# Last FFN: the second product by Strassen's algorithm, with sums made by adding DMAs

## The chip, the cores and the metric

One core of a Trainium2 chip. The metric is the device time of one launch in microseconds (us). The core has engines that run side by side, each with its own queue in program order: TensorE (PE: matmuls, into PSUM), VectorE (DVE), ScalarE (ACT), GpSimd (Pool) and SyncE (SP). DMAs are issued from a queue of SP, ACT or Pool, and are carried by the same 16 DMA engines.

## The reference

A trunk of two layers over 512 tokens of width 1024; each layer is a token mixer and then a dense SwiGLU FFN. The change is in the FFN of the second layer, which is the last thing computed:

```python
D_FF = 2816
def swiglu_ffn(h, w_in, w_out):
    gate, up = jnp.split(h @ w_in, 2, axis=-1)
    return (jax.nn.silu(gate) * up) @ w_out
...
    y = swiglu_ffn(h, f_w_in[i], f_w_out[i])
    x = x + gate * rmsnorm(y, norm_g[i, 3])
```

`h` is [512, 1024], `w_in` [1024, 5632], `w_out` [2816, 1024], all float32. The first product gives gate and up, the second takes their gated product to the output.

## The kernel before

Every operand of a matmul is split in two float32r parts, a high part (a copy that rounds, on ACT) and a low part (the rest, a subtraction on DVE), and each product is three matmuls: high x high, high x low, low x high. The moving operand is 512 wide.

The first product runs over 44 chunks of 128 columns of `w_in` (22 of gate, 22 of up). Each chunk (`in_chunk`) is 8 blocks of the contraction x 3 matmuls into one PSUM bank, with `h` as moving operand. The weights come by SP's queue (`load_w`, 1 MB each, two buffers `wst`) and are split into tiles `whl` (four buffers, `split_w`). `ff_act` makes silu(gate) x up and splits it into 22 tiles `ff`.

The second product is made by `out_begin` and `out_finish`: 2 halves of the output (512 columns) x 22 blocks of the contraction x 4 tiles of 128 tokens x 3 matmuls (`mm_tiles`, lines 378 to 380), the activations as stationary operand. Weights come by `load_wo` (L233) and are split at L203 and L204. The last blocks are left for `finish`, where each token tile is ended in turn (`m0 sq0 b1 yg0 m1a m1b sq1 yg1 rt1 rc1 x0 x1`): squares of the row on ACT (L427), root (L441, ACT) and reciprocal (L444, DVE), product with the gate (L431, DVE), the update of x (L448, DVE) and the store (L450, L457). In this stage the order on PE, ACT and DVE is the program's; elsewhere in `ffn` a scheduler orders them. Pool does nothing here. The launch line gives Pool's DMA descriptors a scratch of 1024 bytes per partition (`dynamic_dma_scratch_size=1024`).

## Time and profile before

| | |
|---|---|
| median of 3 runs | 1366.4 us (1366.18 to 1366.81) |
| profiled execution: its time / its span | 1366.3 us / 1364.5 us |
| TensorE busy | 1353.1 us (99%) |
| DVE / ACT / Pool busy | 849.5 / 539.6 / 11.6 us |
| last FFN, second product: first to last matmul | 1238.54 to 1357.99 us |
| last matmul's end to the span's end | about 1358.4 to 1364.5 us |

The span runs from the first to the last instruction. Rows of groups give line, engine, operation, output<-inputs, shapes and count, then busy time and the mean duration of one in ns, then the idle time ahead of them and what ended it. Durations of matmuls overlap, so their pace is read from start to start. Rows of stretches give the busy time of PE, PE's weight loads, DVE, ACT and Pool with counts, then the granted clock of TensorE (1.00 is full), the mean busy share of the DMA engines, and what they moved in GB/s. Rows of the timeline give start, duration, engine, line and operation.

### The profile page before, as it was taken

What the parts mean: (1) busy time and instruction counts of PE and PEld (TensorE: products, weight loads), DVE (VectorE), ACT (ScalarE), POOL (GpSimd) and SP (SyncE); (2) the same over time, 40 slices, a digit from 0 to 9 for tenths busy, and PEclk for the clock granted to TensorE, in tenths of its full rate; (3) what the DMA queues carried; (4) which work ended last, traced back from release to release, by engine and by line L of the source; (5) the groups of instructions that cost most, each with busy time, mean ns of one, the idle gap of its engine ahead of it and who ended that gap; (6) DMA issues with size and microseconds to landing.
All of it is one profiled execution on the core that took longest, in us unless ns stands there. A gap on an engine that the chain in (4) does not pass through costs nothing.

```text
span 1364.5 us, 17280 instructions
## 1 busy us (share of the span) xinstructions
PE 1353.1 (99%) x6975; PEld 1139.0 (83%) x6975; DVE 849.5 (62%) x1344; ACT 539.6 (40%) x826; POOL 11.6 (1%) x23
## 2 busy tenths in 40 slices
PE   8999999999999999999999999999999999999998
PEld 6788889888888888898888888888898888888886
DVE  5578766787776322759988898897672333333224
ACT  5333355222322222745655545464572232222112
POOL 0000000000000000000000000000000000000000
PEclk9999999999999999999999999999999999999999
DMA  9767750777776232325343433313502332222221
GB/s 311 233 182 241 230 198 17 251 227 246 223 241 215 97 111 90 108 62 160 108 140 110 138 97 105 131 60 119 184 27 83 107 105 98 93 93 93 93 93 62
DMA packets 154212, 190.35 MB, mean 140 GB/s; under 512 B 5892, under 2 KB 111252, under 8 KB 153108
## 3 DMA queue, kind: packets, MB, share of 16 engines
q1 hardware_dynamic: 149984, 176.34, 40.8%
q10 hardware_dynamic: 4148, 12.90, 3.1%
q8 instruction: 55, 0.90, 0.3%
q14 instruction: 25, 0.20, 0.0%
HBM read 186.98 MB, written 2.24 MB: 139 GB/s over the span
## 4 chain that ended last, share of the span: by engine, by line
PE 97%; SPq 2%; DMA 1%; ACT 0%; DVE 0%; issue 0%; DVEq 0%; ACTq 0%
PE ip L276 18%; PE ip L278 18%; PE ip L277 18%; PE y L378 9%; PE y L380 9%; PE y L379 9%; PE li L276 3%; PE li L278 3%; PE li L277 3%; PE li L756 1%; PE yd L1313 1%; SPq L611 1%; PE yo L1307 1%; PE xtr L494 1%; DMA ada_st<-in_ada_w_dram 1%; PE cb L1252 1%
## 5 line engine op out<-in xcount | busy, mean ns | idle before, releaser
L276 PE MATMUL ip<-h,whl 128*128 128x512 f32 x1096 | 430.8, 393 | 0.2 <-DVE cv L863 0.2
L278 PE MATMUL ip<-h,whl 128*128 128x512 f32 x1096 | 426.8, 389 | 0.0
L277 PE MATMUL ip<-h,whl 128*128 128x512 f32 x1096 | 426.5, 389 | 0.0
L276 PEld LDWEIGHTS ip<-h,whl 128*128 128x128 f32 x1096 | 205.8, 188 | 43.9 <-issue 1.8
L278 PEld LDWEIGHTS ip<-h,whl 128*128 128x128 f32 x1096 | 205.7, 188 | 43.3
L277 PEld LDWEIGHTS ip<-h,whl 128*128 128x128 f32 x1096 | 205.8, 188 | 41.8
L204 DVE TENSOR_TENSOR whlo<-wsto,whlo 128x1024 fp32r<-128x1024 f32 x63 | 76.9, 1224 | 162.8 <-ACT whlo L203 162.7
L222 DVE TENSOR_TENSOR whl<-wst,whl 128x1024 fp32r<-128x1024 f32 x96 | 116.7, 1221 | 59.8 <-ACT whl L221 59.6
L378 PE MATMUL y<-whlo,ff 128*128 128x512 f32 x352 | 137.1, 390 | 0.0
L380 PE MATMUL y<-whlo,ff 128*128 128x512 f32 x352 | 136.9, 389 | 0.0
L379 PE MATMUL y<-whlo,ff 128*128 128x512 f32 x352 | 136.9, 389 | 0.0
L203 ACT CAST whlo<-wsto 128x1024 fp32r<-128x1024 f32 x63 | 65.8, 1051 | 162.6 <-PE y L380 149.5
L204 DVE TENSOR_TENSOR whl<-wst,whl 128x1024 fp32r<-128x1024 f32 (+1 forms) x77 | 72.7, 973 | 87.4 <-ACT whl L203 87.4
L124 DVE SCALAR_TENSOR_TENSOR ada_acc<-ada_st,csil,ada_acc 128x512 f32<-128x512 f32 x140 | 105.0, 750 | 4.0 <-DMA ada_st<-in_ada_w_dram 0.5
L221 ACT CAST whl<-wst 128x1024 fp32r<-128x1024 f32 x96 | 99.8, 1041 | 4.1 <-DMA wst<-in_m_w_in_dram 2.4
L203 ACT CAST whl<-wst 128x1024 fp32r<-128x1024 f32 (+1 forms) x77 | 62.6, 846 | 91.1 <-PE ip L278 39.8
L276 PE MATMUL li<-h,whl 128*128 128x256 f32 x288 | 83.2, 289 | 0.0
L278 PE MATMUL li<-h,whl 128*128 128x256 f32 x288 | 81.6, 283 | 0.0
L277 PE MATMUL li<-h,whl 128*128 128x256 f32 x288 | 81.5, 283 | 0.0
L380 PEld LDWEIGHTS y<-whlo,ff 128*128 128x128 f32 x352 | 66.1, 188 | 13.8
L379 PEld LDWEIGHTS y<-whlo,ff 128*128 128x128 f32 x352 | 66.1, 188 | 13.7
L378 PEld LDWEIGHTS y<-whlo,ff 128*128 128x128 f32 x352 | 66.1, 188 | 13.5
(235 smaller groups left out, 1643.9 us busy)
## 6 DMA issues: line engine op xcount, KB each, us to landing
ada_st<-in_ada_w_dram SPq DMA_DIRECT2D x96, 512.0 KB, 5.1
wst<-in_f_w_in_dram SPq DMA_DIRECT2D x44, 1024.0 KB, 5.2
wsto<-in_f_w_out_dram SPq DMA_DIRECT2D x20, 1024.0 KB, 5.0
wst<-in_m_w_in_dram SPq DMA_DIRECT2D x14, 1024.0 KB, 5.4
wst<-in_m_w_in_dram SPq DMA_DIRECT2D x20, 512.0 KB, 5.3
wst<-in_a_w_in_dram SPq DMA_DIRECT2D x9, 1024.0 KB, 6.0
csb<-cs_d ACTq DMA_DIRECT2D x8, 1024.0 KB, 5.1
wsto<-in_m_w_out_dram SPq DMA_DIRECT2D x7, 1024.0 KB, 6.4
```

What stands on the lines that cost most here:

```text
L124: dve.scalar_tensor_tensor(acc, w, csil[:, k:k + 1], acc, MUL, ADD)
L203: act.copy(dst[:, 0, :nk, :], src)
L204: dve.tensor_tensor(dst[:, 1, :nk, :], src, dst[:, 0, :nk, :].bitcast(F32), SUB)
L221: later.append((lambda sw=sw, w=w: act.copy(w[:, 0, :nk, :], sw), lambda sw=sw, w=w: dve.tensor_tensor(w[:, 1, :nk, :], sw, w[:, 0, :nk, : ...
L222: lambda sw=sw, w=w: dve.tensor_tensor(w[:, 1, :nk, :], sw, w[:, 0, :nk, :].bitcast(F32), SUB)))
L276: pe.matmul(dst, w_at(w, 0, kk), a[:, 0, sl], start=start, stop=False)
L277: pe.matmul(dst, w_at(w, 0, kk), a[:, 1, sl], start=False, stop=False)
L278: pe.matmul(dst, w_at(w, 1, kk), a[:, 0, sl], start=False, stop=stop)
L378: pe.matmul(pst, a[:, 0, tk], wt[:, 0, kk, :], start=k == 0, stop=False)
L379: pe.matmul(pst, a[:, 0, tk], wt[:, 1, kk, :], start=False, stop=False)
L380: pe.matmul(pst, a[:, 1, tk], wt[:, 0, kk, :], start=False, stop=k == K - 1)
L494: pe.transpose(pt[:, j * 256 + t * P:j * 256 + (t + 1) * P], self.xn[2 * hi + t][p // 2][:, c:c + P], ident)
```

## The change

The second product is made by Strassen's algorithm in the form that needs seven products of half the size in each dimension. The contraction is parted by blocks: `a?1` and `b1?` are the even blocks of 128, `a?2` and `b2?` the odd ones, 11 of each ("p"). `a1?` are tokens 0 to 255, `a2?` tokens 256 to 511; `b?1` and `b?2` are the two halves of the output's columns. The seven products (`PRODUCTS`) are walked in 77 pairs of product and p, two pairs to a step, 39 steps; a step is 12 matmuls of 512 columns (2 pairs x 2 token tiles x 3 parts). They add into four pairs of PSUM banks, A, B, C and D (one bank for each of the two token tiles), with A taking four of the seven.

The sums of operands are made in place. Of the activations, two are made by DVE (`s13`), and two by DMAs that add (`add_`, issued by Pool): a11 += s1 when product 0 has split its block, a12 += a11 when product 1 has. Of the weights, all four are made by such DMAs: `t1` (b12 += b11), `t3` (b11 is loaded again with the columns of b12 by SP, then b11 += b22), `t2_` (b22 += b12) and `t4` (b21 += b22). They go by units: p = 0 and 1 together, 2 and 3 together, then each p for itself, nine units. The weights of blocks p = 7 to 10 are loaded into the tiles of `h` once the first product has read these, 16 loads of a quarter each.

`behind(n)` is what is issued behind the matmuls of step n; then the weights of step n + 4 (`w_prep`) and the activations of step n + 3 (`a_prep`) are split, from four `whl` and three `ao` buffers. The first two token tiles (c11, c12) are finished at steps 28 to 30, the last two after the last products. The order on all engines is now the program's in the whole FFN.

```diff
-        def ffn(s, i, begun, act_tile, gg_tile, xn_tile, lead, after):
...
+    PRODUCTS = (("A", "b11", "a11"), ("B", "b21", "a12"), ("C", "b22", "a12"), ("A", "b22", "a11"),
+                ("D", "b12", "s1"), ("A", "b11", "a21"), ("A", "b21", "a22"))
-        actp3 = ph.enter_context(tc.tile_pool(name="actp3", bufs=22, reuse_waits="tile"))
-        ffn(3, 1, begun, lambda n: actp3.tile([P, 2, T], F32R, tag="a", name=n),
-            lambda: actp3.tile([P, D], F32, tag="gg", name="gg", bufs=1), None, None, None)
+        fo = ph.enter_context(tc.tile_pool(name="fo", bufs=3, reuse_waits="tile"))
+        fb = ph.enter_context(tc.tile_pool(name="fb", bufs=1, reuse_waits="tile"))
+        h, lead_ps, rest, more = begun
+        w1, w2 = f_w_in[1], f_w_out[1]
+        NP = NF // 2
+        ws, splits, gates = list(more), [(), ()], {}
+        w2t = [fb.tile([P, 2, 2, D], F32, tag=f"w2t{i}", name=f"w2t{i}") for i in range(2)]
+        w2t += [fb.tile([P, 1, 2, D], F32, tag="w2t2", name="w2t2")]
+        raw = fb.tile([P, NF, T], F32, tag="raw", name="raw")
+        s1t = fb.tile([P, NP, 256], F32, tag="s1t", name="s1t")
+        units = [(0, 1), (2, 3)] + [(p,) for p in range(4, NP)]
+        unit_of = {p: i for i, u in enumerate(units) for p in u}
...
+        def w2_load(i):
+
+            u = units[i]
+            t = w2t[i] if i < 3 else wst_p.tile([P, 1, 2, D], F32, tag="wst", name="w2s")
+            for q in range(len(u)):
+                dma(t[:, q, :, :], w2_rows(u[q])[:, 0])
+            rows_of[i] = (t[:, :, 0, :], t[:, :, 1, :])
...
+        def add_(dst, src):
+            pool.dma_start(dst, src, accum_op=ADD)
...
+        def s13(p, n):
+            dve.tensor_tensor(a_("s1", p, n), a_("a21", p, n), a_("a22", p, n), SUB)
+            dve.scalar_tensor_tensor(a_("a21", p, n), a_("a11", p, n), -1.0, a_("a21", p, n), MUL, SUB)
...
+        even = list(range(NP))
+        odd = [4, 0, 1, 2, 3] + list(range(5, NP))
+        steps = [(i, p) for i in range(7) for p in (odd if i % 2 else even)]
+        NT = (len(steps) + 1) // 2
...
+        def w_prep(n):
+            w = whl_p.tile([P, 2, 2, T], F32R, tag="whl", name="whlo")
+            part = steps[2 * n:2 * n + 2]
+            us = {unit_of[p] for _, p in part}
+            if len(us) == 1 and len(part) == 2:
+                todo = [(slice(0, 2), b_(us.pop(), PRODUCTS[part[0][0]][1]))]
+            else:
+                todo = [(slice(q, q + 1), b_(unit_of[p], PRODUCTS[i][1])[:, units[unit_of[p]].index(p):][:, :1])
+                        for q, (i, p) in enumerate(part)]
+            for sl, srcw in todo:
+                act.copy(w[:, 0, sl, :], srcw)
+                dve.tensor_tensor(w[:, 1, sl, :], srcw, w[:, 0, sl, :].bitcast(F32), SUB)
+            w_of[n] = w
+
+        def a_prep(n):
+            a = fo.tile([P, 2, 2, 256], F32R, tag="ao", name="ao")
...
+                    act.copy(a[:, 0, sl, :], srca)
+                    dve.tensor_tensor(a[:, 1, sl, :], srca, a[:, 0, sl, :].bitcast(F32), SUB)
+            for _, (i, p), m in todo:
+                if i == 0:
+                    add_(a_("a11", p, m), a_("s1", p, m))
+                elif i == 1:
+                    add_(a_("a12", p, m), a_("a11", p, m))
+            a_of[n] = a
+
+        def products(tiles):
+            for sub in range(2):
+                for n in tiles:
+                    for q, (i, p) in enumerate(steps[2 * n:2 * n + 2]):
+                        r = PRODUCTS[i][0]
+                        if r not in bank:
+                            bank[r] = [(mm_ps if r == "C" else aux_ps)(f"c{r}{t}") for t in range(2)]
+                        first = i == {"A": 0, "B": 1, "C": 2, "D": 4}[r] and p == (odd if i % 2 else even)[0]
+                        last = p == (odd if i % 2 else even)[-1]
+                        w, a, tk = w_of[n], a_of[n], slice(sub * P, (sub + 1) * P)
+                        for k, (hl, al) in enumerate(((0, 0), (1, 0), (0, 1))):
+                            pe.matmul(bank[r][sub], a[:, al, q, tk], w[:, hl, q, :],
+                                      start=first and k == 0, stop=last and k == 2, skip_group_check=True)
...
+            def t1(i):
+                add_(b_(i, "b12"), b_(i, "b11"))
+
+            def t3(i):
+                u = units[i]
+                for q, p in enumerate(u):
+                    dma(b_(i, "b11", q), w2_rows(p)[:, 0, 0, T:])
+                add_(b_(i, "b11"), b_(i, "b22"))
+
+            def t2_(i):
+                add_(b_(i, "b22"), b_(i, "b12"))
+
+            def t4(i):
+                add_(b_(i, "b21"), b_(i, "b22"))
...
+                if k in (8, 14, 20):
+                    w2_load((8, 14, 20).index(k))
+                if k in (K - 4, K - 2):
+                    w2_load(3 + (k - K + 4) // 2)
+                if k in (K - 12, K - 10, K - 8):
+                    t1((k - K + 12) // 2)
+                tiles.append(in_chunk(ws[k], h))
...
+                    a_prep(k - K + 2)
+                    w_prep(k - K + 2)
+            up(NF - 1, tiles[-1])
+
+            ht = [hp.tile([P, 1, D], F32, tag=f"h{j}", name=f"w2h{j}") for j in range(KD)]
+            for i in range(5, len(units)):
+                rows_of[i] = (ht[2 * (i - 5)], ht[2 * (i - 5) + 1])
+            for c, r in ((0, 0), (0, 1), (1, 0), (1, 1)):
+                for i in range(5, len(units)):
+                    dma(rows_of[i][r][:, 0, c * T:(c + 1) * T], w2_rows(units[i][0])[:, 0, r, c * T:(c + 1) * T])
+            for n in (2, 3):
+                w_prep(n)
+            a_prep(2)
+            for i in range(3, len(units)):
+                t1(i)
...
+            def behind(n):
+
+                if n == 2:
+                    for i in range(len(units)):
+                        t3(i)
+                for i, u in enumerate(units):
+                    if n - 8 == u[-1] // 2:
+                        t2_(i)
+                if n == 18:
+                    for i in range(len(units)):
+                        t4(i)
+                for t in range(2):
+                    if n == 5:
+                        got["11", t] = t2("c11")
+                        act.copy(got["11", t], bank["A"][t])
+                    elif n == 10:
+                        dve.tensor_add(got["11", t], got["11", t], bank["B"][t])
+                    elif n == 16:
+                        got["12", t] = t2("c12")
+                        act.copy(got["12", t], bank["C"][t])
+                    elif n == 21:
+                        dve.tensor_tensor(got["12", t], got["12", t], bank["A"][t], SUB)
+                    elif n == 27:
+                        dve.tensor_add(got["12", t], got["12", t], bank["D"][t])
+                        got["22", t] = spare[f"c22_{t}"]
+                        act.copy(got["22", t], bank["D"][t])
+                    elif n == 28:
+                        square(t, 0, got["11", t])
+                        square(t, 1, got["12", t])
+                        mean(t)
+                    elif n == 29:
+                        root(t)
+                        for hf, c in enumerate(("11", "12")):
+                            gated(got[c, t], hf, got[c, t])
+                    elif n == 30:
+                        for hf, c in enumerate(("11", "12")):
+                            x_new(t, hf, got[c, t])
+                    elif n == 32:
+                        dve.tensor_tensor(got["22", t], got["22", t], bank["A"][t], SUB)
+                    elif n == 33:
+                        square(2 + t, 0, got["22", t])
+                        mean(2 + t)
+                    elif n == 34:
+                        gated(got["22", t], 1, got["22", t])
+
+            for n in range(NT - 3):
+                products([n])
+                behind(n)
+                if n == 26:
+                    for hf in range(2):
+                        dma(gg[hf], gate_d[3, 4 * hf:4 * hf + 4].rearrange("j p -> (j p)").partition_broadcast(P))
+                if n + 4 < NT:
+                    w_prep(n + 4)
+                if n + 3 < NT:
+                    a_prep(n + 3)
+            products(range(NT - 3, NT))
+            for t in range(2):
+                square(2 + t, 1, bank["A"][t])
+                yg = gated(bank["A"][t], 0, t2("yg"))
+                root(2 + t)
+                if t == 0:
+                    x_new(2, 0, yg)
+                    x_new(2, 1, got["22", 0])
+                else:
+                    x_new(3, 1, got["22", 1])
+                    x_new(3, 0, yg, HALVES, (dma_s, dma))
```

More of the change, by code (lines that the diff above doesn't have):

```diff
@@ L954, in trunk_kernel @@
             begun = out_finish(parts, tail, ws0)
-        def ffn(s, i, begun, act_tile, gg_tile, xn_tile, lead, after):
-            w1, w2 = f_w_in[i], f_w_out[i]
-            acts = []
-            h, lead_ps, rest, more = begun
-            def ff_act(psg, psu, f):
-                g = t2("g")
-                act.activation(g, psg, AF.Silu)
-                dve.tensor_mul(g, psu, g)
-                a = act_tile(f"ff{f}")
-                act.copy(a[:, 0, :], g)
-                dve.tensor_tensor(a[:, 1, :], g, a[:, 0, :].bitcast(F32), SUB)
-                acts.append(a)
-            for f in range(0, NF, 2):
-                if f == 0:
-                    with tc.manual_schedule(engines={PE_ENGINE}):
-                        for i in (0, 2, 1, 3, 4, 5):
-                            rest(i)
-                    pss = lead_ps[:4]
-                elif f == 2:
-                    pss = lead_ps[4:] + [in_chunk(w, h) for w in more]
-                else:
-                    pss = [in_chunk(w, h) for w in load_w([(w1, f * P, 256)]) + load_w([(w1, DFF + f * P, 256)])]
-                for b in range(2):
-                    ff_act(pss[b], pss[2 + b], f + b)
-                if f == 18:
-                    gg = make_gg(s, gg_tile)
-            return out_finish(out_begin(s, w2, lambda k: acts[k], NF, [gg], xn_tile, "aux", lead, after))
         def ssd_lead():
```

80 lines of the change are left out of this document (added).

## The prediction

> **What bounds the kernel now.** I read the page's first and fourth part, then the stretches of the last FFN, then single matmuls.
>
> ```profile
> PE 1353.1 (99%) x6975; PEld 1139.0 (83%) x6975; DVE 849.5 (62%) x1344; ACT 539.6 (40%) x826; POOL 11.6 (1%) x23
> PE 97%; SPq 2%; DMA 1%; ACT 0%; DVE 0%; issue 0%; DVEq 0%; ACTq 0%
> 1250.00:1300.00 50.00, 50.00 (x223) 41.38 (x222) 11.37 (x10) 10.21 (x10) 0.00 (x0) 1.00 0.31 106
> ```
>
> TensorE is 97% of the chain that ended last, and in the second product (third row: one stretch of it) it is busy for all 50 us, at full clock, with DVE and ACT at a fifth and the DMA engines at 0.31. So a matmul removed here is time removed, and the other engines have room. What is a matmul worth? The groups give 389 ns each, but these spans overlap. The timeline tells the pace:
>
> ```profile
> 1238.54 0.39 PE L378 MATMUL y<-whlo,ff 128*128 128x512 f32 x1
> ...
> 1357.99 0.39 PE L380 MATMUL y<-whlo,ff 128*128 128x512 f32 x1
> L378 PE MATMUL y<-whlo,ff 128*128 128x512 f32 x176 | 68.5, 389 | 0.0
> ```
>
> The first and the last of 3 x 176 = 528 matmuls start 119.45 us apart, so one costs 119.45 / 527 = 0.2267 us.
>
> **Part 1: the matmuls.** Before: 22 blocks of the contraction x 4 token tiles x 2 halves x 3 = 528. After: 7 products x 11 blocks x 2 token tiles x 3 = 462, all 512 wide as before, so the same 0.2267 us. 66 fewer: -15.0 us. At 389 ns it would read -25.7; that is not time. The products come in 39 steps of 12 matmuls (2.72 us; the last has 6).
>
> **Part 2: splitting.** Each step now needs its weights and its activations split.
>
> ```profile
> L203 ACT CAST whlo<-wsto 128x1024 fp32r<-128x1024 f32 x22 | 23.2, 1053 | 86.2 <-PE y L380 74.5 <-issue 7.8 <-PE ip L278 3.9
> L204 DVE TENSOR_TENSOR whlo<-wsto,whlo 128x1024 fp32r<-128x1024 f32 x22 | 27.0, 1225 | 84.4 <-ACT whlo L203 84.4
> L967 ACT CAST ff<-g 128x512 fp32r<-128x512 f32 x22 | 13.5, 617 | 0.0
> L968 DVE TENSOR_TENSOR ff<-g,ff 128x512 fp32r<-128x512 f32 x22 | 15.0, 685 | 2.5 <-ACT ff L967 2.5
> ```
>
> Weights are 128x1024 per step, as one instruction or two of 512; activations 128x512. ACT: up to 3 x 0.617 = 1.85 us, DVE: up to 3 x 0.685 = 2.06 us of each 2.72. Hidden while nothing else is on DVE's queue; four weight tiles and three activation tiles put this work about three steps (8 us) ahead, which is its cover. Cost: 0, while the inputs are there. The sums that DVE makes in the first product (two of 128x512 for each four blocks) replace splits it made there: 0.
>
> **Part 3: the adds by DMA, and the queue they stand in.** The trace has no DMA on Pool's queue, and no DMA that adds. What I can follow is the order. Step 11 (t = 11 x 2.72 = 29.9 us after the first product's last matmul) is the first to read a12 as changed. Its split is ACT 0.62 + DVE 0.69, so the sum must have landed by 28.6. On Pool's queue, in program order, there stand before that sum: `t1` of the six units 3 to 8, seven blocks of a11, then at step 2 all nine `t3`, then a11 of block 10 and a12 of block 4. `t3` for its part waits for 11 reloads on SP's queue, which stand behind 16 quarter loads into the old h tiles, and those cannot start before the last first-product chunk lets h go (eight k of three matmuls, so from about t = -4.8). All this is wanted by step 27 only (`t3`), but is moved ahead of what step 11 needs.
>
> Bytes, at 128x512x4 = 262 kB a half row block: SP 27 x 262 kB = 7.08 MB. Pool: `t1` 6 x 262, `t3` 11 x 262, a11 seven and a12 three blocks of 131 kB = 5.77 MB. The rate: 24 to 40 us into the kernel the loads come without a break.
>
> ```profile
> DMA  9999999999999999999999999999999999999999
> DMA packets 5773, 5.58 MB, mean 349 GB/s; under 512 B 278, under 2 KB 5771, under 8 KB 5771
> L450 SPq DMA_DIRECT2D out_dram<-x x7: 332/332/366, 1349.5 to 1360.8; - x7
> DMA to landing us min/median/max: 2.0/2.1/2.2
> ```
>
> 349 GB/s is what the engines give; a 256 KB transfer lands 2.1 us after its issue, and I count two such landings in series at the end (last reload to its add; the a12 sum itself).
>
> Price of an add, in copies of the same bytes: below, nothing, if adds ran wholly beside the loads; a gain is excluded, as no transfer is taken away. Above, two copies (it reads two streams). A copy reads one stream and writes one, an add reads two and writes one: three movements for two, so I take 1.5. Then (7.08 + 1.5 x 5.77) MB / 349 GB/s = 45.1 us; from -4.8 that is 40.3, with two landings 44.5, against 28.6: TensorE waits 15.9 us at step 11. At price 1 the same sum gives 36.2, a wait of 7.6; at 2 it gives 52.8, a wait of 24.2; at 0 there is none (SP's bytes alone are through at 15.5).
>
> [...]
>
> What issuing costs Pool: SP's row says 0.33 us for one; for Pool's own queue no row exists, and the longest instruction Pool runs here is this:
>
> ```profile
> L1329 POOL TENSOR_TENSOR accg<-accg,sqg 128x512 f32<-128x512 f32 x7 | 9.1, 1299 | 879.1 <-ACT sqg L1327 879.1
> ```
>
> 21 adds up to and with the sum that step 11 needs, from t = 5 on, at 0.33 to 1.3 us each are 7 to 27 us, so issued by 12 to 32: under the 40 us of the bytes. I take 0 on top.
>
> After the wait the later adds (`t2_` for step 16, `t4` for step 33) have had all that time and are early.
>
> A wait of this length has its own cost. Rows of the tail, where TensorE has stopped at 1358.4:
>
> ```profile
> 1358.00:1361.00 3.00, 0.38 (x2) 0.00 (x0) 1.77 (x4) 0.98 (x3) 0.00 (x0) 0.95 0.31 115
> 1361.00:1364.50 3.50, 0.00 (x0) 0.00 (x0) 0.53 (x2) 0.00 (x0) 0.00 (x0) 0.50 0.43 150
> ```
>
> The clock falls to half some 2.3 us after the last matmul. How long it stays there when work comes back no row shows: 0 to 2 us of delay, I take 1. [...]
>
> **Part 4: finishing the first two token tiles inside the products.** At steps 27 to 30 DVE's queue gets, ahead of the splits of later steps, work that stood in the tail or between tiles before:
>
> ```profile
> L431 DVE TENSOR_TENSOR yg<-y,gg 128x512 f32<-128x512 f32 x8 | 5.5, 686 | 4.6 <-ACT junk L427 4.6
> L448 DVE SCALAR_TENSOR_TENSOR x<-yg,ss,x 128x512 f32<-128x512 f32 x10 | 7.1, 748 | 0.2
> L427 ACT ACTIVATE junk<-y 128x512 f32<-128x512 f32 x8 | 4.8, 596 | 13.8 <-PE y L380 13.8
> L441 ACT ACT_TABLE_LOAD x1 | 1.3, 1283 | 0.0
> L444 DVE RECIPROCAL ss<-ss 128x1 f32<-128x1 f32 x4 | 0.6, 156 | 0.9 <-ACT ss L441 0.9
> ```
>
> DVE: two adds and four gatings (6 x 0.69), four x updates (4 x 0.75), means and reciprocals (4 x 0.15) = 7.7 us. It also waits about 3 us: four squares stand on ACT (4 x 0.6) before the second mean, and a table load (1.28) before the first root. The splits of five steps are 5 x 2.06 = 10.3. Together 21 us from the end of step 27, where step 33 is due five steps or 13.6 us later; instructions that follow each other overlap by about 0.1 us (some 25 of them), which leaves 18.5. Then TensorE waits about 5 us at steps 32 and 33, because the split that step needs stands behind all this. Bounds: 0 (if the queue has its full 8 us lead) and 7.4. I take 5.
>
> **Part 5: the end.** After the last matmul one token tile is left, with the same chain as before (square, root, reciprocal, gated product, three x pieces, two stores: 1358.38 to 1364.5). The other tile of the pair finishes beside the last 15 matmuls (3.4 us). 0, or up to 0.5 either way.
>
> **Sum.** The profiled execution took 1366.3 us (span 1364.5 and 1.8 around it), 0.1 below the median of 1366.4. -15.0 + 15.9 + 1 + 5 = +6.9 on it: 1373.2, and with the 0.1 to the median 1373.3.
>
> **Rivals.**
>
> A. The adds hide. If the engines move adds beside loads (price up to about 0.5, since the loads' 349 GB/s may be a limit of the memory they read and not of the engines), nothing waits at step 11: at 0.5 the sum lands at 28.0. Then -15.0 + 5 = -10: 1356.4, or 1351.4 if DVE keeps its lead too. For it: DMA share 0.31 before, nothing but SBUF is touched by an add. Against it: the sum at price 1 is already late, and the share at 349 GB/s is full.
>
> B. Slower still: Pool's queue passes adds one by one. If each add waits for the landing of the one before, 21 adds x 2.1 us = 44 us from t = 5, or nearer 55 at 2.6 us each with the added read: step 11's sum lands at 49 to 60, a wait of 20 to 31 us. It decides once an add takes over 1.9 us on the queue (39.5 us up to my 44.5, over 21). -15 + 5 + 1 + 20 to 31 = +11 to +22, and more if `t2_` is late as well: 1377 to 1395. Price 2, the upper bound of part 3, falls in the same band, at 1382. For it: no row shows Pool with several transfers under way. Against it: SP holds several at once.
>
> C. No difference: price near 1 and a wait of 7.6: -15 + 7.6 + 1 + 5 = -1.4, 1365. Between the forecast and A.
>
> **How the numbers follow.** A measurement of this kernel tells 0.2% (2.7 us) from no change. My case (price 1.2 to 1.8, net +2 to +12) has 0.40, A 0.33, B with price 2 has 0.20, C 0.07. Faster by over 0.2%: A and a part of C, 0.36. Same: the rest of C and the lower edge of mine, 0.05. Slower 0.59. The likeliest case alone spans 1368 to 1378; both signs hold much of the chance, so the range takes in most of A and B: 1354.5 to 1394.
>
> **What would show it.** Right: one wait of TensorE at the 12th step (about 30 us into the products), released through ACT and DVE by a DMA add on a12; Pool's queue still busy with `t3` then; a smaller wait at the 33rd or 34th step, released by DVE; 462 matmuls at 0.227 us. Wrong: no idle before that step (A), or an add of 262 kB that takes well under 0.6 us or over 1.5 us of the engines, or waits spread over every step, which would mean that splitting and not the adds is the bound.

## The result, and the profile after

| | before | after |
|---|---|---|
| median | 1366.47 us (1366.18 to 1366.81) | 1413.99 us (1412.52 to 1415.56) |
| span of the profiled execution | 1364.5 us | 1413.2 us |

The ratio is 1.0348 [1.033, 1.0366]: 47.5 us slower, where the prediction had +6.9 us and a range that ended at 1394. The sign was right, the size was not.

The page of the changed kernel, first, third and fourth part, and the group of the third product's matmuls:

```profile
PE 1348.6 (95%) x6909; PEld 1132.0 (80%) x6909; DVE 892.0 (63%) x1436; ACT 570.1 (40%) x893; POOL 60.0 (4%) x71
q0 software_dynamic: 9216, 14.42, 6.2%
PE 89%; issue 5%; POOL 2%; DMA 1%; DVE 1%; SPq 1%; ACT 1%; DVEq 0%; POOLq 0%; ACTq 0%
L1661 PE MATMUL cC<-whlo,ao 128*128 128x512 f32 x66 | 21.6, 485 | 47.5 <-ACT ao L1639 47.5
```

The matmuls that were to go are gone (6975 before, 6909 now). But TensorE's share of the chain fell from 97% to 89%, and "issue" (5%) and Pool (2%) stand on it, though Pool is busy for 4% of the span. One group tells where: TensorE sat idle for 47.5 us ahead of the third product, bank C, the first that reads a12 as changed. The waits of the last FFN give the whole chain; columns are the total, the number, and the longest:

```profile
PE cC L1661 <- ACT ao L1639: 47.5, 4, 32.7
ACT ao L1639 <- DMA raw<-raw: 43.8, 4, 36.4
ACT whlo L1622 <- DMA w2t<-w2t: 15.0, 1, 15.0
PE cA L1661 <- DVE w2h L1787: 4.3, 1, 4.3
```

TensorE waits for ACT's split of the activations, and that for the adding DMA into a12 (raw<-raw): 32.7 us at step 11. In the same 47.5 us hides a second long wait. The timeline of TensorE has it:

```profile
1301.40 7.71 PE L1661 MATMUL cC<-whlo,ao 128*128 128x512 f32 x24 [32.75 <-ACT ao L1639]
...
1330.43 6.45 PE L1661 MATMUL cC<-whlo,ao 128*128 128x512 f32 x15 [13.37 <-ACT ao L1639]
...
1382.61 2.54 PE L1661 MATMUL cA<-whlo,ao 128*128 128x512 f32 x10 [2.01 <-DVE ao L1640]
1389.49 17.51 PE L1661 MATMUL cA<-whlo,ao 128*128 128x512 f32 x66 [4.35 <-DVE w2h L1787]
```

At the second wait TensorE stands ahead of step 15, and the activations of that step are named as the releaser. But on ACT's queue they come behind the weights of step 16, and for these ACT itself waited 15.0 us, for a sum of weights (w2t<-w2t, `t2_`):

```profile
1329.24 0.62 ACT L1622 CAST whlo<-w2t 128x512 fp32r<-128x512 f32 x1 [15.01 <-DMA w2t<-w2t]
1329.77 0.61 ACT L1639 CAST ao<-raw 128x512 fp32r<-128x512 f32 x1
```

It is called the wait for step 16 below, after the sum that was late. The last two waits are at steps 32 and 33.

Why are the sums late? Before the long wait the DMA engines are full, but in it they are not. These are a stretch ahead of it and two stretches of it (busy time of PE, PEld, DVE, ACT and Pool, then the clock, the DMA share and GB/s):

```profile
1250.00:1260.00 10.00, 10.00 (x46) 8.29 (x45) 7.15 (x11) 7.18 (x13) 3.21 (x4) 1.00 1.10 300
1270.00:1280.00 10.00, 0.00 (x0) 0.00 (x0) 0.00 (x0) 0.00 (x0) 2.90 (x3) 0.58 0.49 79
1280.00:1290.00 10.00, 0.00 (x0) 0.00 (x0) 0.00 (x0) 0.00 (x0) 5.08 (x7) 0.50 0.87 149
```

And this is Pool's timeline in and behind the wait:

```profile
1274.01 1.21 POOL L1581 DMA_DIRECT2D w2t<-w2t  x1 [2.94 <-issue]
1279.38 2.14 POOL L1581 DMA_DIRECT2D w2t<-w2t  x2 [4.16 <-issue]
...
1288.38 0.86 POOL L1581 DMA_DIRECT2D w2h<-w2h  x1 [0.99 <-issue]
1289.94 0.88 POOL L1581 DMA_DIRECT2D w2h<-w2h  x1 [0.71 <-issue]
...
1296.82 1.22 POOL L1581 DMA_DIRECT2D raw<-raw  x1 [1.45 <-issue]
1300.99 1.21 POOL L1581 DMA_DIRECT2D raw<-raw  x1 [2.96 <-issue]
1305.12 1.22 POOL L1581 DMA_DIRECT2D raw<-raw  x1 [2.92 <-issue]
1309.26 1.21 POOL L1581 DMA_DIRECT2D raw<-raw  x1 [2.91 <-DVE whlo L1623]
```

While TensorE, DVE and ACT stand still, Pool issues adds with long gaps, and the two-row adds of a12 behind them every 4.14 us: 1.2 us of work, 2.9 us of "issue", that is, of waiting for nothing that the trace shows. The adds into w2h come 1.4 to 1.6 us apart. Both kinds move 256 KB. What differs is the shape: an add of a12 covers two rows of its tile (two pieces of 128 partitions), one of w2h a single row of 512 columns. The view of the DMA queues for 1290 to 1320 us shows the engines stop between the adds, and how long one takes:

```profile
DMA  9999999891059600099100497000991005960009
raw<-raw POOLq DMA_DIRECT2D x5, 256.0 KB, 3.8
```

3.8 us from issue to landing, and the next is issued 0.3 us later: the two-row adds go strictly one after the other.

The account, from the first to the last matmul of the second product: 119.45 us before, 168.0 after (1238.6 to 1406.6), +48.55. 66 matmuls fewer are -15.0. The waits are 32.75 + 13.37 + 1.37 (two short ones at steps 13 and 14) + 6.36 = +53.85. The remaining +9.7 is matmuls that ran slower, for the most part behind the waits, where the granted clock is 0.50.

### The profile page after: what moved, and what is told of

It reads as the page before. It is cut to its first block, busy times and chain, and to the rows that moved or that the text cites. A ratio compares the mean times of both kernels' runs of the same rounds, so it can differ in the third digit from the quotient of the medians.

```text
span 1413.2 us, 17451 instructions
## 1 busy us (share of the span) xinstructions
PE 1348.6 (95%) x6909; PEld 1132.0 (80%) x6909; DVE 892.0 (63%) x1436; ACT 570.1 (40%) x893; POOL 60.0 (4%) x71
## 3 DMA queue, kind: packets, MB, share of 16 engines
q0 software_dynamic: 9216, 14.42, 6.2%
## 4 chain that ended last, share of the span: by engine, by line
PE 89%; issue 5%; POOL 2%; DMA 1%; DVE 1%; SPq 1%; ACT 1%; DVEq 0%; POOLq 0%; ACTq 0%
PE ip L276 18%; PE ip L278 17%; PE ip L277 17%; PE y L378 6%; PE y L380 6%; PE y L379 6%; PE li L276 2%; PE li L278 2%; PE li L277 2%; PE cA L1661 2%; PE li L756 2%; PE yd L1283 1%; PE cD L1661 1%; PE yo L1277 1%; PE xtr L494 1%
## 5 line engine op out<-in xcount | busy, mean ns | idle before, releaser
L222 DVE TENSOR_TENSOR whl<-wst,whl 128x1024 fp32r<-128x1024 f32 x132 | 160.7, 1221 | 133.4 <-ACT whl L221 133.1
L221 ACT CAST whl<-wst 128x1024 fp32r<-128x1024 f32 x132 | 136.6, 1042 | 32.5 <-PE ip L278 23.7
L204 DVE TENSOR_TENSOR whlo<-wsto,whlo 128x1024 fp32r<-128x1024 f32 x41 | 49.9, 1224 | 78.9 <-ACT whlo L203 78.8
L203 ACT CAST whlo<-wsto 128x1024 fp32r<-128x1024 f32 x41 | 42.6, 1049 | 76.4 <-PE y L380 70.5
L1661 PE MATMUL cA<-whlo,ao 128*128 128x512 f32 x264 | 64.0, 401 | 6.4 <-DVE w2h L1787 4.3
L378 PE MATMUL y<-whlo,ff 128*128 128x512 f32 x176 | 68.6, 390 | 0.0
L380 PE MATMUL y<-whlo,ff 128*128 128x512 f32 x176 | 68.5, 389 | 0.0
L379 PE MATMUL y<-whlo,ff 128*128 128x512 f32 x176 | 68.5, 389 | 0.0
L1661 PE MATMUL cC<-whlo,ao 128*128 128x512 f32 x66 | 21.6, 485 | 47.5 <-ACT ao L1639 47.5
L1661 PEld LDWEIGHTS cA<-whlo,ao 128*128 128x128 f32 x264 | 50.9, 194 | 18.5 <-issue 4.7
L1142 DVE SCALAR_TENSOR_TENSOR cu<-ip,cols,cu 128x511 f32<-128x511 f32 (+2 forms) x84 | 62.8, 747 | 3.9 <-ACT cu L1139 1.4
L1588 ACT ACTIVATE g<-ip 128x512 f32<-128x512 f32 x18 | 10.8, 598 | 122.3 <-PE ip L278 122.3
```

Of the source, the lines that this page charges most:

```text
L204: dve.tensor_tensor(dst[:, 1, :nk, :], src, dst[:, 0, :nk, :].bitcast(F32), SUB)
L221: later.append((lambda sw=sw, w=w: act.copy(w[:, 0, :nk, :], sw), lambda sw=sw, w=w: dve.tensor_tensor(w[:, 1, :nk, :], sw, w[:, 0, :nk, : ...
L222: lambda sw=sw, w=w: dve.tensor_tensor(w[:, 1, :nk, :], sw, w[:, 0, :nk, :].bitcast(F32), SUB)))
L378: pe.matmul(pst, a[:, 0, tk], wt[:, 0, kk, :], start=k == 0, stop=False)
L379: pe.matmul(pst, a[:, 0, tk], wt[:, 1, kk, :], start=False, stop=False)
L380: pe.matmul(pst, a[:, 1, tk], wt[:, 0, kk, :], start=False, stop=k == K - 1)
```

## Experiments

The medians of before beside these runs were 1366.26 to 1366.51 us. Waits are read from TensorE's timeline, as above.

**1. No adds.** `add_` issues nothing: the operands stay unsummed.

```diff
-            pool.dma_start(dst, src, accum_op=ADD)
+            pass
```

> The changed kernel with every adding DMA left out (the reloads of b11 stay; the sums are missing from the operands). Theory, that the adds alone make the two long waits: no wait of TensorE at steps 11 and 16, the one of about 6 us near steps 32 and 33 (DVE's queue) stays, so 1366.4 - 15.0 + 6 = 1357 us. Rival, that splitting seven products' operands or SP's loads hold TensorE too: waits remain spread over the steps, 1365 us or more.

Measured: 1360.85 us (1359.87 to 1361.51), ratio 0.9956 [0.994, 0.9973]. The timeline of TensorE:

```profile
1328.80 2.59 PE L1661 MATMUL cA<-whlo,ao 128*128 128x512 f32 x10 [2.02 <-DVE ao L1640]
1335.68 17.93 PE L1661 MATMUL cA<-whlo,ao 128*128 128x512 f32 x66 [4.29 <-DVE w2h L1787]
```

No wait is left ahead of step 32, so the splits hide, and the whole of the loss ahead of that step hangs on the adds: 53 us. What stays is -5.6 us: -15.0 for the matmuls and some +9.4 for the finishing work on DVE's queue, 6.3 of it waits and the rest matmuls at a lower clock (0.73 on average from 1330 to 1340 us). The expectation of 1357 had the waits and left out these slower matmuls.

**2. Twice the descriptor space.** The `dynamic_dma_scratch_size` of the launch line, below called the descriptor space, is 2048 bytes in place of 1024; two small tiles make room by standing in scratch tiles. Order and bytes are those of after.

```diff
-dynamic_dma_scratch_size=1024
+dynamic_dma_scratch_size=2048
```

> The changed kernel with 2048 instead of 1024 bytes per partition for the descriptors of Pool's DMAs (room made by two small constants put elsewhere); nothing else. Theory, that the adds of two rows per partition go one by one because only one of them fits into the descriptor space: the space between two such adds on Pool's queue falls from 4.1 to 5.3 us to 1.5 to 2.5 us, the wait at step 11 from 36 to 15 to 25 us, that at step 16 from 15 to under 6, and the time from 1414 to 1380 to 1395. Rival, that the DMA engines need this time for the bytes of an add: spacing and time as in the changed kernel, 1410 to 1416.

Measured: 1385.49 us (one run), 28.5 less than after. The wait at step 11 falls from 32.75 to 20.42 us, that for step 16 from 13.37 to 1.12. Pool's timeline:

```profile
1282.13 1.20 POOL L1582 DMA_DIRECT2D raw<-raw  x1 [1.60 <-issue]
1284.59 1.20 POOL L1582 DMA_DIRECT2D raw<-raw  x1 [1.25 <-issue]
1286.56 1.22 POOL L1582 DMA_DIRECT2D raw<-raw  x1 [0.77 <-issue]
```

the view of the DMA queues for 1281 to 1291 us, and a stretch of the wait that is left:

```profile
raw<-raw POOLq DMA_DIRECT2D x5, 256.0 KB, 4.4
...
1270.00:1280.00 10.00, 0.00 (x0) 0.00 (x0) 0.00 (x0) 0.00 (x0) 6.49 (x8) 0.64 1.13 217
```

The same two-row adds now come 2.0 to 2.5 us apart. Each takes 4.4 us from issue to landing here, so two are on their way at a time, where after had one. The DMA engines are full (1.13 where after had 0.49). So the space set the pace in the kernel after; once it is doubled, the engines do, and this is the wait that the prediction's sum of bytes describes. No view shows the descriptors themselves: that those of one two-row add fill the 1024 bytes is the author's conclusion from this run (4.14 us between adds, 2.0 to 2.5 with 2048) and from experiment 9.

**3. Copies in place of adds.** The same transfers without the addition, so the operands are not sums.

```diff
-            pool.dma_start(dst, src, accum_op=ADD)
+            pool.dma_start(dst, src)
```

> The changed kernel with the same transfers on Pool's queue as plain copies (no add: the destination is overwritten, so the operands are not the sums). Theory, that an add costs the engines two copies: the queue's share of 16 engines falls from 6.2% of 1413 us (88 us) to about half (44 us), and as a copy also needs fewer descriptors the two-row transfers no longer go one by one; 1370 to 1390. Rival, that an add costs the engines what a copy does and the waits come from the issue on Pool: share 6%, spacing 4 us, time within 10 us of 1414.

Measured: 1369.16 us (one run), a wait of 6.54 us at step 11 and none for step 16. The queue's row for the same 14.42 MB, here and (above) after:

```profile
q0 software_dynamic: 4288, 14.42, 2.9%
```

6.2% of the span of 1413.2 us is 87.6 us of the engines for adds, 2.9% of the 1367.3 us here is 39.7 us for copies: an add costs 2.2 copies. The adds also went in more packets, 9216 against 4288, so whether the bytes or the packets make the price stays open. The time of this run tells nothing of the price by itself, as two-row copies do not go one by one: they stand 1.0 to 1.3 us apart with the same 1024 bytes. Pool's issue is shorter as well, 0.54 us for one row and 0.72 for two, where an add takes 0.87 and 1.2.

**4. The sums by GpSimd.** No DMA at all for them.

```diff
-            pool.dma_start(dst, src, accum_op=ADD)
+            pool.tensor_tensor(dst, dst, src, ADD)
```

> The changed kernel with each sum made by GpSimd's own tensor_tensor instead of an adding DMA (same order, same places). By the one row before, 128x512 in 1.30 us: 28.6 us of Pool from t = 5 to the sum that step 11 needs, a wait of about 5 us there, under 3 at step 16, about 6 near step 32: 1366.4 - 15 + 5 + 3 + 6 = about 1365 us. Rival, that GpSimd and DVE get in each other's way at SBUF: DVE's splits take visibly longer than 0.685 and 1.225 us or Pool's adds longer than 1.3 us, waits over many steps, 1380 us or more.

Measured: 1397.07 us (1396.5 to 1399.24), ratio 1.0227 [1.0211, 1.0242]: better than after, still slower than before, and what the rival gave. A group of DVE's splits behind the first product, first of this kernel (1255 to 1330 us), then of experiment 1 (1255 to 1320 us), which makes the same splits beside an idle Pool:

```profile
L1640 DVE TENSOR_TENSOR ao<-raw,ao 128x512 fp32r<-128x512 f32 x15 | 23.6, 1572 | 4.4 <-ACT ao L1639 4.4
```

```profile
L1640 DVE TENSOR_TENSOR ao<-raw,ao 128x512 fp32r<-128x512 f32 x17 | 11.6, 684 | 0.0
```

and a group of Pool in this kernel:

```profile
L1581 POOL TENSOR_TENSOR w2h<-w2h 128x512 f32<-128x512 f32 x8 | 13.9, 1766 | 0.0
```

A split that takes 0.68 us alone takes 1.57 us beside an adding GpSimd, and GpSimd's own addition 1.77 where the kernel before showed 1.30. DVE has 2.06 us of splits for each step of 2.72; stretched 2.3 times they no longer fit, and TensorE waits for them in most steps of the second to the fourth product. These rows show that the two slow each other here; they do not show through what.

**5 and 6. The order of use, with 1024 and with 2048 bytes.** `t1` of units 3 to 8 goes to steps 0, 1 and 4, and all `t3` from step 2 to step 14, with their second term read from DRAM and their reloads issued at step 12.

```diff
-            for i in range(3, len(units)):
-                t1(i)
...
-                if n == 2:
+                for i in {0: (3, 4), 1: (5, 6), 4: (7, 8)}.get(n, ()):
+                    t1(i)
+                if n == 12:
+                    for i in range(len(units)):
+                        t3_load(i)
+                if n == 14:
                     for i in range(len(units)):
                         t3(i)
```

> The changed kernel (1024 bytes of descriptor space) with the adds issued in the order in which they are due: t1 of units 3 to 8 at steps 0, 1 and 4, the reloads for t3 at step 12 and its adds at step 14, behind t2 (its second term then comes straight from the weights in memory, as b22 is changed by then). Same adds, same bytes. Theory, that step 11 waited because of what stood ahead of its sum: no wait at step 11; the queue as a whole is still slow (two-row adds 4 to 5 us each), so about 15 us appear at step 16, which needs t2: 1366.4 - 15 + 9 (DVE near step 32, as in e1) + 15 = about 1375 us. Rival, that order matters little and the DMA engines are behind from the start: a wait of 20 us or more at step 11 remains, 1390 us or more.

> Order of e5 and the 2048 bytes of e2 together. Theory, that order and descriptor space are two separate causes that add: no wait at steps 11 and 16, only DVE's near step 32, as with no adds at all: 1361 us, up to 1366 if the engines (an add counted as two copies, about 92 us of work at 349 GB/s beside 104 us of products) are late for single steps. Rival, that the engines are the limit whatever the order: waits of 10 us or more move to later steps, 1372 us or more.

Measured: 1389.3 us (one run) with 1024 bytes; 1371.18 us (1370.14 to 1372.38) with 2048, ratio 1.0033 [1.0021, 1.0045]. With 1024 bytes the wait at step 11 is down to 6.21 us, so the order of the queue was worth 26.5 us of it, but the wait for step 16 is still 13.35: the two-row adds of a12 stand 4.1 us apart in front of `t2_`, whatever comes first. The expectation of 1375 had this second wait. What it left out are the 6.21 us, 2.64 us of short waits at steps 12 to 14, and most of the 10.8 us by which matmuls ran slower. With both changes the two waits are 2.21 and 3.51 us; with 2.0 and 2.8 us of slower matmuls behind them they make up the 10 us that experiment 6 lies above experiment 1, where none were expected or, at the most, 5.

**7 and 8. The finishing work spread out, without adds and with all sums.** Squares and means of the first half go to steps 11 and 12, the four gatings one to a step (28 to 31), and the x updates of the first two tiles to the end of the loop. Experiment 8 is 6 with this.

```diff
-                    elif n == 30:
-                        for hf, c in enumerate(("11", "12")):
-                            x_new(t, hf, got[c, t])
...
+                if n in (28, 29, 30, 31):
+                    hf, t = divmod(n - 28, 2)
+                    c = ("11", "12")[hf]
+                    gated(got[c, t], hf, got[c, t])
+                if n in (11, 12):
+                    square(n - 11, 0, got["11", n - 11], t2("junk"))
+                    mean(n - 11)
...
+            for t in range(2):
+                gated(got["22", t], 1, got["22", t])
+                for hf, c in enumerate(("11", "12")):
+                    x_new(t, hf, got[c, t])
             products(range(NT - 3, NT))
```

> e1 (no adds; the sums are missing from the operands) with the finishing work of the first two token tiles spread: squares of c11 at steps 11 and 12, the four products with the gate at steps 28 to 31 one by one, the four updates of x behind the last split. Theory, that DVE's queue at steps 27 to 30 makes the wait near step 32, which with the clock's fall costs about 9 us in e1: the wait goes, 1361 - 9 = 1352 us, which is 66 matmuls less and nothing else. Rival, that the wait comes from the splits themselves being too many for DVE: 1358 us or more.

> Order, descriptor space and spread tail together, all sums in place. If the three causes add: 1366.4 - 15.0 = 1351.5 us and up to 4 us of waits of single steps, so 1352 to 1356 us, below the kernel before. Rival, that the adds' engine time shows once nothing else does: 1360 us or more.

Measured: 1356.05 us (1355.78 to 1356.72) without adds, ratio 0.9924 [0.991, 0.9937]; 1365.53 us (1364.65 to 1366.93) with all sums, ratio 0.9993 [0.9984, 1.0002], no difference to before. Both lie above their expectations, by 4 and by some 10 us. Experiment 7 has one wait, at step 33, for the subtractions of bank A, which stand on DVE's queue behind the splits of later steps:

```profile
1331.25 16.81 PE L1661 MATMUL cA<-whlo,ao 128*128 128x512 f32 x66 [2.66 <-DVE w2h L1780]
```

66 matmuls at 0.2267 us take 15.13 us with the last one's 0.39; here they take 16.81, so a wait of 2.66 us costs 1.7 us more behind it. Experiment 8 has three such waits (2.71, 2.49 and 2.67 us, at step 11, for step 16 and at step 33). Its time is that of the rival; experiments 10 to 12 show that the rival's reason, the engines' time for the adds, is not the cause.

**9. One row per add.** The kernel after, 1024 bytes and its own order, with each two-row add issued as two.

```diff
-            pool.dma_start(dst, src, accum_op=ADD)
+            for q in range(dst.shape[1]):
+                pool.dma_start(dst[:, q, :], src[:, q, :], accum_op=ADD)
```

> The kernel after with its 1024 bytes of descriptor space and its order, but every add that covers two rows of a tile (two 128-partition pieces) issued as two adds of one row each: same bytes, same descriptors in total, more instructions. Theory (the descriptors of ONE instruction fill the space, so a two-row add must drain before the next may be written, 4.14 us apart, while one-row adds stand 1.3 to 1.5 us apart): a pair costs 2.6 to 3.0 us in place of 4.14 (5.3 for a w2t pair), so some twelve pairs ahead of the sum of step 11 save 1.1 to 2.3 us each: the wait at step 11 falls from 36 us to about 20, that of step 16 from 15 to about 10, and the time is about 1392 us. Rival (each add costs its own drain whatever its size): 22 more adds at 1.3 us or more on top, a wait at step 11 of 36 us or more, time 1414 us or above. Rival (bytes alone set the pace): no change, 1414 us.

Measured: 1392.65 us (1392.64 to 1392.66), ratio 1.0191 [1.0172, 1.021]. More instructions, the same bytes, 21 us less than after, as expected; the waits at step 11 and for step 16 are 24.48 and 3.65 us, where about 20 and 10 were expected. Pool's timeline:

```profile
1288.92 2.65 POOL L1582 DMA_DIRECT2D raw<-raw  x3 [0.75 <-issue]
1291.94 2.77 POOL L1582 DMA_DIRECT2D raw<-raw  x3 [0.37 <-issue]
```

and the queue's row for 1270 to 1300 us:

```profile
q0 software_dynamic: 3341, 4.49, 94.3%
```

Two rows of a12 go in 2.0 us in place of 4.14. So neither their bytes nor their number made the two-row adds serial. What is left is the size of one add against the space, as concluded in experiment 2. The queue's row prices an add once more: 4.49 MB in 94.3% of 30 us is 159 GB/s of sums, against the prediction's 349 GB/s of loads, 2.2 times the engines' time.

**10 to 12. What was left of experiment 8.** In 10 the reloads of b11 (which SyncE had issued some 20 us early, so that they shared the DMA engines with the adds, at a share of 1.13 and 1.15 from 1250 to 1270 us of experiment 8) are issued by ACT at step 13, and at step 32 the subtractions of bank A stand ahead of the splits. The adds of `t3` and `t4`, which come behind `t2_` on Pool's queue, also move, from steps 14 and 18 to 18 and 20:

```diff
-                    dma(b_(i, "b11", q), w2_rows(p)[:, 0, 0, T:])
+                    act.dma_start(b_(i, "b11", q), w2_rows(p)[:, 0, 0, T:])
...
+                if n == 32:
+                    a_prep(34)
+                    w_prep(35)
-                if n + 4 < NT:
+                if n + 4 < NT and n != 31:
```

> All sums in place, with 2048 bytes, the adds in the order of their use, and the finishing work spread (1365.5 us so far, three waits of 2.5 to 2.7 us at steps 11, 16 and 33, each followed by about 3.4 us of half clock). Two edits more: the reloads of the first half of the weight rows, which SyncE issues about 20 us before they are needed, are issued by ScalarE between its splits of steps 17 and 18, so that they cannot use the DMA engines while the sums of steps 11 to 16 are in flight; and at the 32nd step the two subtractions of bank A stand on VectorE ahead of the splits of steps 34 and 35. Theory (the sums of steps 11 and 16 land late only because the reloads share the DMA engines with them; the wait at step 33 is only the place on VectorE's queue): all three waits go, each is worth 2.6 us and about 1.7 us of half clock, and the time is 1365.5 - 13 = 1352 to 1356 us, below the kernel before (1366.4). Rival (Pool's descriptor space still sets the pace of the adds): the waits at steps 11 and 16 stay, only the third goes, 1361 us. Rival (ScalarE's queue is held by the issues): new waits on the splits, 1365 us or more.

Measured: 1366.91 us (1365.69 to 1368.09), ratio 1.0002 [0.9993, 1.0011]. The wait at step 11 is gone and that at step 33 is 0.86 us. But the sum for step 16 is still late: TensorE stands 2.08 us ahead of step 15, though no reload was issued before that sum had landed. So the theory held for step 11 and not for step 16. And the last rival came in: ACT's queue was held by the issues.

```profile
1280.66 5.69 ACTq L1677 DMA_DIRECT2D w2t<-in_f_w_out_dram  x4
1293.34 2.09 PE L1662 MATMUL cC<-whlo,ao 128*128 128x512 f32 x3 [7.37 <-ACT ao L1640]
```

Four issues took 5.69 us there, all eleven 11.6 us, and the splits behind them came late: a new wait of 7.37 us at step 16.

In 11 SyncE issues the reloads again, held by a transfer of two numbers that reads the copy of bank C (step 16), and `t2_` of unit 2, which step 16 needs first, goes ahead of those of units 0 and 1, which answers the 2.08 us:

```diff
+                        if t == 0:
+                            dma(st[3]["s2"][:1, :2], got["12", 0][:1, :2])
+                            for i in range(len(units)):
+                                t3_load(i)
...
+                for i in {9: (2, 0, 1), 10: (3,), 11: (4, 5), 12: (6, 7), 13: (8,)}.get(n, ()):
+                    t2_(i)
```

> The kernel of the run before (1366.9 us; the wait at step 11 gone, but waits of 2.1 and 7.4 us at steps 15 and 16 behind eleven issues of about 1.1 us each on ScalarE) with the eleven reloads back on SyncE, held there by a transfer of two numbers that reads the copy of the third product's sum (step 16), so that they start at about 1285 us; and with the sum of weights that step 16 needs first (unit 2) put ahead of those of units 0 and 1 on GpSimd's queue. Theory (the adds themselves fit behind the matmuls once the reloads are out of their way and their order is that of use; ScalarE's issues alone made the new waits): no wait at steps 11 and 16, 0.9 us at step 33, time 1366.9 - 9.5 of waits - about 4 of half clock = 1353 to 1356 us, faster than before (1366.4). Rival (the adds alone saturate the DMA engines and set the pace): the sum of step 16 still lands late, 2 to 4 us of wait with its half clock, 1358 to 1363 us. Rival (the held reloads are now late for the sums of the sixth product): a new wait near step 27, 1360 us or more.

Measured: 1359.4 us (1357.56 to 1360.19), ratio 0.995 [0.9936, 0.9963]; there is no wait at step 11 or for step 16. But this `t2_` stood one step too early: the third product took the sum of unit 2 where it should take the row, and TensorE waited 3.25 us for it, ahead of step 12 and for the weights of step 13, a wait that none of the theories had. Experiment 12 puts it one step later, behind that split, and changes nothing else:

```diff
-                for i in {9: (2, 0, 1), 10: (3,), 11: (4, 5), 12: (6, 7), 13: (8,)}.get(n, ()):
+                for i in {10: (2, 0, 1, 3), 11: (4, 5), 12: (6, 7), 13: (8,)}.get(n, ()):
```

> The kernel of the run before with the sum of unit 2 one step later, at the 11th step in place of the 10th, so that it stands behind the split of the same row for the third product (in the run before, the third product took the sum there in place of the row, and TensorE waited 3.25 us for it at step 13). Nothing else is changed: 2048 bytes of descriptor space, adds in the order of use, reloads held to step 16, spread finishing work, all sums in place. Theory (the adds fit behind the matmuls once they stand in their order and alone on the DMA engines): the wait of 3.25 us at step 13 and about 1.7 us of half clock behind it go, and only 0.9 us at step 33 is left: 1359.4 - 5 = 1354.4 us, between 1353 and 1357, faster than before by about 12 us. Rival (the adds are paced by their bytes: the same sum is then late at step 16): a wait of 2 us or more there, 1357 to 1362 us.

Measured: 1353.0 us (1352.84 to 1353.23), ratio 0.9903 [0.9886, 0.9919], 13.3 us faster than before and 61 faster than after. The page's first row:

```profile
PE 1339.8 (99%) x6909; PEld 1127.6 (83%) x6909; DVE 892.1 (66%) x1436; ACT 570.5 (42%) x893; POOL 60.3 (4%) x71
```

and TensorE's timeline:

```profile
1268.69 14.44 PE L1662 MATMUL cC<-whlo,ao 128*128 128x512 f32 x63
...
1329.55 15.21 PE L1662 MATMUL cA<-whlo,ao 128*128 128x512 f32 x66 [0.86 <-DVE w2h L1786]
```

The third product, which waited 47.5 us, now runs without a gap, and one wait of 0.86 us is left of all. The last row also says that this short wait left the clock alone: 15.21 us for the 66 matmuls against 15.13, at a granted clock of 1.00 from 1330 to 1340 us.

## Why the prediction was wrong in size

**Part 1, the matmuls: right.** In experiment 12 the first and the last matmul of the second product start 105.6 us apart (1238.8 to 1344.4), where before had 119.45: -13.85, which is the -15.0 with the 0.86 of step 33 and some small gaps given back. The pace is unchanged: 63 matmuls in 14.44 us, the last one's 0.39 counted whole.

**Part 2, the splits hidden: right while Pool only issues DMAs.** Experiment 1 ahead of step 32 and experiment 12 as a whole show no wait on a split that had its inputs in time. With the sums on Pool itself (experiment 4), where a split took 1.57 us in place of 0.68, the cover was gone.

**Part 3, the adds: the place was right, the mechanism was not.** TensorE waited at the 12th step, through ACT, for an adding DMA on a12, with `t3` ahead of it on Pool's queue, as written. The wait was 32.75 us, not 15.9, and three steps of the sum were at fault:

- "I take 0 on top" for issuing. This is the step that failed. Pool's queue did not run ahead of the bytes: two-row adds went one at a time, at 4.1 us each (5.3 to 5.4 for 512 KB), which experiments 2 and 9 put down to the descriptor space, and the DMA share was 0.49 in a stretch in which I had the engines full. That is rival B's mechanism, at about twice the 1.9 us per add from which it would decide, and for the two-row adds alone, which the prediction did not tell from the rest. Rival B's bounds for the wait (20 to 31 us) nearly hold 32.75. Doubling the space alone took 12.3 us off this wait and as much off the one for step 16 (experiment 2).
- The price of 1.5 copies, the author's estimate from what an add reads and writes; no run showed an add by then. Experiments 3 and 9 both give 2.2, a little past its upper bound of two. At 159 GB/s an add of 262 kB takes 1.65 us of the engines, past the 1.5 us that the prediction named as a sign of being wrong. At price 2 the prediction's sum gave a wait of 24.2 us, and experiment 2, where the engines set the pace, has 20.42; at price 1 it gave 7.6, and experiment 3 has 6.54.
- The later adds, which the prediction called early. The wait for step 16, for `t2_`, was 13.37 us. The queue was late as a whole, so the first wait gave no lead: behind the sum of step 11 (issued at 1296.82) stood four more two-row adds of a12 at 4.1 us, and then the `t2_` of units 0 and 1 at 5.3, ahead of the `t2_` of unit 2 that step 16 needs. Experiment 5 has 13.35 us with the first wait cut to 6.21, and experiment 2 has 1.12: it is the spacing again.

**The clock term of 1 us**, a choice between 0 and 2 that no row gave, was for the first wait alone. Behind its 32.75 us, 24 matmuls took 7.71 us in place of 5.60, a loss of 2.1; behind the 13.37 us, 15 took 6.45 in place of 3.56, a loss of 2.9; and a wait of 2.66 us cost 1.7 (experiment 7). In the kernel after, slower matmuls come to 9.7 us in all. In slices of 1 us of the kernel after the granted clock was 0.50 from the return at 1301.4 us to 1305 and 0.67 in the slice behind that, and 0.50 from the return at 1330.4 to 1336 and 0.81 in the slice behind that: an estimated 4.3 and 6.0 us at half, if the clock was either 0.50 or 1.00. In experiment 7 its mean from 1330 to 1340 us was 0.83, by the same estimate 3.4 us at half, and half of that is the 1.7 lost. Idle times of 2.5 to 2.7 us were enough here for such a loss (experiments 7 and 8; 15 matmuls behind the 2.49 us took 5.22 in place of 3.56). In experiment 9 so were 2.01 us (10 matmuls in 4.14 us), though in the kernel after the same 2.01 us were not (10 in 2.54 us).

**Part 4, DVE's queue: right in place, half right in mechanism.** The waits at steps 32 and 33 are 2.01 + 4.35 = 6.36 us (predicted 5, bounds 0 to 7.4); with the clock behind them experiment 1 has 9.4. Step 32 waited for its split behind the finishing work, as written. At step 33 the split (the first row) was done at 1386.95 us; TensorE went on at 1389.49, behind the first of two subtractions of bank A (the second row), which stand behind three more splits:

```profile
1386.26 0.69 DVE L1640 TENSOR_TENSOR ao<-raw,ao 128x512 fp32r<-128x512 f32 x1
...
1388.66 1.28 DVE L1787 TENSOR_TENSOR w2h<-w2h,cA 128x512 f32<-128x512 f32 x2
```

The prediction's list of DVE's work has no such subtraction, so that the size came out near 5 is in part luck. Put ahead of the splits, it leaves 0.86 us of that wait (experiments 10 and 12).

**Part 5, the end: right within its 0.5.** From the last matmul's start to the end of the span there are 6.51 us in the kernel before, 6.59 after and 6.53 in experiment 12.

**Rivals.** A (the adds hide) is what the change does once order, space, reloads and finishing work are mended: its lower figure was 1351.4, experiment 12 has 1353.0. But its reason, a price of 0.5 or less, is not the one: the price is 2.2, and the adds hide because each is issued in time. As the change stands, A fell, by the price of an add and by the space. C needed a price near 1 and fell with it.

## What to carry to other kernels

Before work is moved to a queue that looks idle, count what one instruction needs of that queue's own resources, and not only its bytes: here two-row adds went one by one, at 4.1 us for 256 KB with 1024 bytes of descriptor space and 2.0 to 2.5 us with 2048, while the DMA engines stood half idle in a part of the wait (a share of 0.49) and Pool read 4% busy. "issue" of nearly constant length (2.9 us) between equal DMA instructions is how that looked in the timeline; doubling the space (28.5 us) and one row per add (21 us) are cheap tests. On one queue the order of use can be worth as much as the space (26.5 us of one wait here), and loads that ran ahead of need took the DMA engines from what was needed first (2.71 us at step 11, experiments 8 and 10).

## What the runs showed of the hardware that was not expected

- An adding DMA costs Pool 0.87 us to issue for one row of 128 partitions and 1.2 us for two, a copy 0.54 and 0.72.
- With 1024 bytes of descriptor space two-row adds of the same shape stand 4.14 us apart, with 2048 bytes 2.0 to 2.5 us, and one-row adds of the same 256 KB 1.4 to 1.6 us at 1024.
- Adds moved 159 GB/s within SBUF (experiment 9), where loads from DRAM moved 349 (the kernel before).
- DVE's subtraction of 128x512 took 0.68 us alone and 1.57 us on average beside GpSimd's additions.
- Eleven issues of 256 KB loads held ACT's queue for 11.6 us, up to 1.4 us each, in a stretch with the DMA share at 1.09.
